# Layer B's attention: probabilities transposed one key block ahead of their products, work for later head pairs in smaller parts

## The chip, the cores and the metric

The kernel runs on one core of one Trainium2 chip. The metric is the time of one execution on the device in microseconds (us). The core's engines are TensorE (PE in the profile; PEld is its weight load), VectorE (DVE), ScalarE (ACT), GpSimd (POOL) and SyncE (SP); each runs its own instructions in their order and waits for the others at semaphores.

## What is computed

A trunk of two layers over 1024 tokens of width 1024: layer A (sparse attention and an MLP), then layer B (attention with shared keys and values, and an MLP). The change touches the attention of layer B alone:

```python
k_shared, v_shared = mla_shared_kv(rms_norm(h, kv_norm), w_dkv, ...)   # 16 heads, keys 96 wide, values 64 wide
...
q = (rms_norm(h @ w_dq, q_lora_gain) @ w_uq).reshape(b, s, B_HEADS, QK_DIM)
q = rope_tail(rms_norm(q, q_gain), cos, sin)
logits = jnp.einsum('bqhd,bshd->bhqs', qb, k).astype(jnp.float32) * (QK_DIM ** -0.5)
logits = jnp.where(mask, logits, NEG)          # key chunk of 64 not later than the query's
p = jax.nn.softmax(logits, axis=-1).astype(v.dtype)
out = jnp.einsum('bhqs,bshd->bqhd', p, v)
```

Products are float32 in effect: an operand is split into a high and a low part, and each product is made of two or three matmuls.

## The kernel before

The 16 heads of layer B go in eight pairs j = 0 to 7. A pair has four **quarters** (half, h): half 0 are queries 0 to 511, half 1 queries 512 to 1023, and h is the head of the pair. They go in the order (0,0), (1,0), (0,1), (1,1) (the last pair ends with (1,1), (0,1)).

For each quarter `logits` makes four rows of blocks, i = 0 to 3: scores of 128 queries against their admissible keys (tile `blps`, L938, two PSUM banks in turn), their negated copy with the least value on VectorE (`bpr`, L939), the exponential on ScalarE (L942), the reciprocal of the sum on VectorE (L943), and the scaling on GpSimd (L944). `values` then goes over the quarter's key blocks sb (4 for half 0, 8 for half 1): up to four transposes of probabilities into a PSUM bank `bpt` (L957), a copy of the high part on ScalarE (`bph`, L88), the low part on VectorE (`bpl`, L88), and two products with the values into `bpo` (L962), first that of the high part, then that of the low. `output` adds the quarter into `res` with a copy `btmp` on ScalarE (L971) and an add on VectorE (L972).

The loop runs `logits` of a quarter beside `values` of the quarter before it, step by step, and strews between them the quarter's list in `plan`: work for later pairs, which is one long step each. `kv_a` makes keys and values of 256 tokens (12 matmuls into `pukv`, L750; copies and four squares with their sums on ScalarE, `ksq`; a root on GpSimd, `y_bk`, L81; scaling into `ktok` on VectorE). `kv_b` transposes them (`pkt`, L775). `q_a` makes queries of 256 tokens (18 matmuls into `puq`, L794; a copy and four squares on ScalarE, `bqsq`), `q_b` norms and rotates 512 of them (`y_bq` and three products of `qtok` on GpSimd, L813 to L818), `queries_t` transposes them (`pqt`, L825). Transposes of probabilities and this work share four PSUM banks (tag `pt`).

The code is not the order on the chip: the program is built with a scheduler that places the written steps anew on every engine, by its own estimate of their durations (`schedule_with_timeline_sim`). What stands where is therefore shown below from the built program.

## Time and profile before

| what | value |
|---|---|
| median of 3 runs | 2685.81 us (2684.93 to 2688.60) |
| the profiled execution, its own time | 2684.85 us |
| its span from first to last instruction | 2683.0 us |
| mean granted clock of TensorE | 0.984 |
| TensorE busy | 2532.4 us (94%), 13354 matmuls |
| its weight loads busy | 2148.5 us (80%) |
| VectorE busy | 1521.1 us (57%) |
| ScalarE busy | 1232.2 us (46%) |
| GpSimd busy | 1024.1 us (38%) |

The profile is of one execution. An engine's busy time is the union of its instructions. A matmul's end is modelled, so that a busy TensorE is not one at its peak. Idle time is put down to what ended last. The attention of layer B stands at 1446 to 1888 us of the span.

### The profile page before, as it was taken

To read this page: it belongs to the slowest core of one execution; us is meant where nothing else is said; L and a number is where in the kernel's file an instruction comes from. 1 tells how busy PE (TensorE), PEld (TensorE's weight loads), DVE (VectorE), ACT (ScalarE), POOL (GpSimd) and SP (SyncE) were. 2 spreads that over 40 slices of the span, in tenths; PEclk is the share of its full clock that TensorE was granted. 3 is DMA by queue.
4 is the path that set the end of the run, shared out by engine and by line. 5 is a ranking of instruction groups with operands and counts; after the bars stand their busy time and mean duration, and the time that the engine had idled before them with its cause. 6 is when DMAs were issued, how large, how long until landed. Compare 5 with 4: busy or idle time off the path is not lost.

```text
span 2683.0 us, 36853 instructions
## 1 busy us (share of the span) xinstructions
PE 2532.4 (94%) x13354; PEld 2148.5 (80%) x13354; DVE 1521.1 (57%) x3655; ACT 1232.2 (46%) x2989; POOL 1024.1 (38%) x756
## 2 busy tenths in 40 slices
PE   6997799999989999999998999998999999999999
PEld 5897678888768888888888788887778888888887
DVE  5798754999869861222257878897422232222223
ACT  4575744333357764243345777787222222222221
POOL 2235635443556535343324555555121212222120
PEclk9998999999999999999999999999999999999999
DMA  7202323222232223233210000002210101111111
GB/s 157 54 24 60 99 92 97 94 99 90 79 110 68 60 82 127 84 120 106 77 33 11 10 14 10 14 5 80 102 32 32 63 32 63 47 48 48 48 47 63
DMA packets 122293, 173.03 MB, mean 64 GB/s; under 512 B 12752, under 2 KB 101104, under 8 KB 122112
## 3 DMA queue, kind: packets, MB, share of 16 engines
q1 hardware_dynamic: 122112, 170.69, 20.5%
q8 instruction: 105, 1.72, 0.3%
q14 instruction: 76, 0.62, 0.1%
HBM read 159.13 MB, written 11.53 MB: 64 GB/s over the span
## 4 chain that ended last, share of the span: by engine, by line
PE 71%; DVE 7%; DMA 3%; ACT 3%; POOL 2%; issue 2%; SPq 0%; POOLq 0%; DVEq 0%; ACTq 0%
PE pd L1190 25%; PE pu L1120 25%; PE pwo L1066 3%; PE pwoa L1066 2%; PE blps L938 2%; PE bpo L962 2%; PE puq L794 2%; PE po L572 1%; PE ppt L566 1%; PE lps L543 1%; PE pcq L853 1%; PE pukv L750 1%; DVE bpr L939 1%; PE bpt L957 1%; PE pck L853 1%
## 5 line engine op out<-in xcount | busy, mean ns | idle before, releaser
L88 POOL TENSOR_TENSOR dl<-rd,dh 128x1024 fp32r<-128x1024 f32 x96 | 232.4, 2429 | 728.2 <-PE pu L1120 369.3
L1191 DVE TENSOR_TENSOR res<-res,pd 128x1024 f32<-128x1024 f32 x192 | 234.2, 1220 | 419.1 <-PE pd L1190 419.1
L1120 PE MATMUL pu<-mxh,uh 128*128 128x512 f32 (+1 forms) x1056 | 405.4, 384 | 2.4 <-DVE mxl L88 2.4
L1120 PE MATMUL pu<-mxl,uh 128*128 128x512 f32 (+1 forms) x1056 | 404.9, 383 | 0.0
L1120 PE MATMUL pu<-mxh,ul 128*128 128x512 f32 (+1 forms) x1056 | 404.9, 383 | 0.0
L1190 PE MATMUL pd<-dh,hh 128*128 128x512 f32 x1024 | 398.6, 390 | 5.1 <-DVE res L1191 3.1
L1190 PE MATMUL pd<-dl,hh 128*128 128x512 f32 x1024 | 398.5, 389 | 0.0
L1190 PE MATMUL pd<-dh,hl 128*128 128x512 f32 x1024 | 392.9, 389 | 1.6 <-DVE hl L88 1.6
L88 DVE TENSOR_TENSOR hl<-pu,hh 128x512 fp32r<-128x512 f32 (+1 forms) x132 | 88.8, 674 | 407.6 <-ACT hh L88 407.6
L88 ACT CAST dh<-rd 128x1024 fp32r<-128x1024 f32 x96 | 99.1, 1051 | 476.1 <-PE pd L1190 422.5
L88 POOL TENSOR_TENSOR ul<-ru,uh 128x1024 fp32r<-128x1024 f32 x96 | 231.9, 2418 | 167.2 <-ACT uh L88 166.9
L1177 ACT ACTIVATE pu<-pu 128x512 f32<-128x512 f32 (+1 forms) x132 | 75.0, 569 | 433.2 <-PE pu L1120 427.7
L1120 PEld LDWEIGHTS pu<-mxh,uh 128*128 128x128 f32 x1056 | 199.1, 189 | 41.7 <-DVE mxl L88 2.9
L1120 PEld LDWEIGHTS pu<-mxl,uh 128*128 128x128 f32 x1056 | 198.9, 188 | 39.0
L1120 PEld LDWEIGHTS pu<-mxh,ul 128*128 128x128 f32 x1056 | 199.0, 188 | 38.7
L1190 PEld LDWEIGHTS pd<-dh,hh 128*128 128x128 f32 x1024 | 192.3, 188 | 46.5 <-DVE res L1191 4.0
L1190 PEld LDWEIGHTS pd<-dh,hl 128*128 128x128 f32 x1024 | 192.2, 188 | 42.1 <-DVE hl L88 2.2
L1190 PEld LDWEIGHTS pd<-dl,hh 128*128 128x128 f32 x1024 | 192.3, 188 | 39.7
L444 DVE TENSOR_SCALAR_CACHE_REDUCE both<-score,cand 128x1024 f32<-128x1024 f32 (+1 forms) x192 | 181.2, 944 | 5.0
L944 POOL TENSOR_SCALAR bpr<-bpr,bsm 128x640 f32<-128x640 f32 (+7 forms) x128 | 98.4, 772 | 96.4 <-DVE bsm L943 55.9
L554 POOL TENSOR_SCALAR lg<-lg,sm 128x256 f32<-128x256 f32 (+7 forms) x128 | 99.4, 783 | 76.7 <-DVE sm L553 54.0
L88 ACT CAST uh<-ru 128x1024 fp32r<-128x1024 f32 x96 | 99.9, 1044 | 30.4 <-DMA ru<-in_mlp_w_up_dram 28.4
(374 smaller groups left out, 5982.0 us busy)
## 6 DMA issues: line engine op xcount, KB each, us to landing
ru<-in_mlp_w_up_dram SPq DMA_DIRECT2D x48, 1024.0 KB, 5.4
rd<-in_mlp_w_down_dram SPq DMA_DIRECT2D x48, 1024.0 KB, 4.9
bm<-near_d SPq DMA_DIRECT2D x56, 256.0 KB, 2.7
res<-in_x_dram SPq DMA_DIRECT2D x16, 512.0 KB, 6.3
wor_a<-in_a_w_o_dram SPq DMA_DIRECT2D x16, 512.0 KB, 3.6
wr_q<-in_a_w_in_dram SPq DMA_DIRECT2D x8, 512.0 KB, 8.7
x<-res SPq DMA_DIRECT2D x8, 512.0 KB, 2.6
wor_b<-in_b_w_o_dram SPq DMA_DIRECT2D x8, 512.0 KB, 3.6
```

The costliest lines, as they stand in the source:

```text
L88: return self.nc.scalar.copy(h, src), (engine or self.nc.vector).tensor_sub(l, src, h)
L444: nc.vector.tensor_scalar(scratch[0][0][:, :s.shape[-1]], s, cand[:, j:j + 1], None, op0=ALU.is_ge, op1=ALU.add, accum_out=cnt[:, j:j + 1])
L554: nc.gpsimd.tensor_scalar(lg[:, :S], lg[:, :S], rs, 1.0, op0=ALU.mult, op1=ALU.mult)
L794: nc.tensor.matmul(ps[:, 192 * u:192 * u + 192], a[:, kb, tsl], b[:, kb], start=(kb == 0 and i == 0), stop=(kb == 2 and i == 2))
L853: nc.tensor.matmul(ps, a[:, kb], b[:, kb], start=(kb == 0 and i == 0), stop=(kb == KB - 1 and i == 2))
L938: nc.tensor.matmul(lps, q[0:rows, tsl], k[0:rows, h, c:c + a], start=(m == 0), stop=(m == 2))
L944: nc.gpsimd.tensor_scalar(pr, pr, sm[:, 3:4], 1.0, op0=ALU.mult, op1=ALU.mult)
L1066: nc.tensor.matmul(open_ps[n], x[:, kb], w[:, kb, ns], start=(kb == 0 and i == 0), stop=(kb == KB - 1 and i == 2))
L1120: nc.tensor.matmul(pu, a[:, kb], b[:, kb, c0:c1], start=(kb == 0 and i == 0), stop=(kb == KB - 1 and i == 2))
L1177: nc.scalar.activation(pu, pu, AF.Relu)
L1190: nc.tensor.matmul(pd[:, ns], a[:, tsl], b[:, ns], start=(f == 0 and k == 0), stop=(f == NS - 1 and k == 2))
L1191: nc.vector.tensor_add(res[:, tb], res[:, tb], pd)
```

## The change

`values` is cut in two: `turn_probs` makes the transposes of a key block and their high and low parts, and `values` only the two products. `attended` writes the steps of a quarter: the transposes of key block sb + 1 stand ahead of the products of block sb, and a share of the other work stands between the two. `bph` and `bpl` have three buffers in place of two. `kv_a` and `q_a` go in two parts (128 tokens each), so that other steps may stand between their halves; copies and squares come behind the second part. The lists of `plan` are spread anew over the four quarters, and the last quarter's products are written with the output projection between them in the same manner. The number of instructions on each engine stays.

```diff
@@ -739,17 +739,21 @@
                 keys[j] = stream(w_ukv[:, :, 256 * j:256 * j + 256], 2, 256, "uk", j, 1)
                 vals[j] = (a2 if j % 2 else j2).tile([P, NB, 2, P], F32R, name=f"bv{j}", tag="bv", bufs=1)
 
-            def kv_a(j, t2):
+            def kv_a(j, t2, parts=(0, 1)):
 
                 wh, wl = keys[j]
-                ps = filler((2, 2, P), f"pukv{j}_{t2}")
-                for u in range(2):
+                if 0 in parts:
+                    keys["ps", j, t2] = filler((2, 2, P), f"pukv{j}_{t2}")
+                ps = keys["ps", j, t2]
+                for u in parts:
                     tsl = slice((2 * t2 + u) * P, (2 * t2 + u + 1) * P)
                     for kb in range(2):
                         for i, (a, b) in enumerate(((ckh, wh), (ckh, wl), (ckl, wh))):
                             nc.tensor.matmul(ps[:, 256 * u:256 * u + 256], a[:, kb, tsl], b[:, kb],
                                              start=(kb == 0 and i == 0), stop=(kb == 1 and i == 2))
-                ps = ps.rearrange("p (a b c) -> p a b c", a=2, b=2)
+                if 1 not in parts:
+                    return
+                ps = keys.pop(("ps", j, t2)).rearrange("p (a b c) -> p a b c", a=2, b=2)
                 kt = j2.tile([P, 2, 2, 96], F32, name=f"ktok{j}_{t2}", tag="ktok", bufs=3)
                 ss = j2.tile([P, 2, 2], F32, name=f"bkss{j}_{t2}", tag="bkss")
                 nc.scalar.copy(kt[:, :, :, 0:64], ps[:, :, :, 0:64])
@@ -779,20 +783,25 @@
             def q_w(j):
                 keys["q", j] = stream(w_uq[:, :, 192 * j:192 * j + 192], 3, 192, "uq", j, 2)
 
-            def q_a(j, t2):
+            def q_a(j, t2, parts=(0, 1)):
 
                 half = t2 // 2
-                if t2 % 2 == 0:
+                if t2 % 2 == 0 and 0 in parts:
                     qtok[j, half] = j2.tile([P, 4, 2, 96], F32, name=f"qtok{j}_{half}", tag="qtok", bufs=4)
                     sums[j, half] = j2.tile([P, 4, 2], F32, name=f"bqss{j}_{half}", tag="bqss", bufs=4)
                 wh, wl = keys["q", j]
-                ps = filler((2, 192), f"puq{j}_{t2}")
-                for u in range(2):
...
+                if 1 not in parts:
+                    return
+                del keys["qs", j, t2]
                 b = 2 * (t2 % 2)
                 q = qtok[j, half][:, b:b + 2]
                 nc.scalar.copy(q, ps.rearrange("p (u h c) -> p u h c", u=2, h=2))
@@ -944,29 +953,48 @@
                 nc.gpsimd.tensor_scalar(pr, pr, sm[:, 3:4], 1.0, op0=ALU.mult, op1=ALU.mult)
                 probs[j, half, h, i] = pr
 
-            def values(j, half, h, sb):
+            parts = {}
+
+            def turn_probs(j, half, h, sb):
+
                 nm = f"{j}_{half}_{h}"
-                nb = 4 * half + 4
-                if sb == 0:
-                    outs[j, half, h] = pp.tile([P, 512], F32, name=f"bpo{nm}", tag="po", bufs=2)
-                po = outs[j, half, h]
                 i0 = max(0, sb - 4 * half)
                 c = slice(i0 * P, 512)
                 pt = pp.tile([P, 4, P], F32, name=f"bpt{nm}_{sb}", tag="pt", bufs=4)
                 for i in range(i0, 4):
                     nc.tensor.transpose(pt[:, i], probs[j, half, h, i][:, sb * P:(sb + 1) * P], self.ident)
-                ph = a2.tile([P, 512], F32R, name=f"bph{nm}_{sb}", tag="bph")
-                pl = a2.tile([P, 512], F32R, name=f"bpl{nm}_{sb}", tag="bpl")
+                ph = a2.tile([P, 512], F32R, name=f"bph{nm}_{sb}", tag="bph", bufs=3)
+                pl = a2.tile([P, 512], F32R, name=f"bpl{nm}_{sb}", tag="bpl", bufs=3)
                 self.split_evac(ph[:, c], pl[:, c], pt.rearrange("p a b -> p (a b)")[:, c])
-                for n, m in enumerate((ph, pl)):
+                parts[j, half, h, sb] = ph, pl
+
+            def values(j, half, h, sb):
+                nb = 4 * half + 4
+                if sb == 0:
+                    outs[j, half, h] = pp.tile([P, 512], F32, name=f"bpo{j}_{half}_{h}", tag="po", bufs=2)
+                po = outs[j, half, h]
+                c = slice(max(0, sb - 4 * half) * P, 512)
+                for n, m in enumerate(parts.pop((j, half, h, sb))):
                     nc.tensor.matmul(po[:, c], vals[j][:, sb, h], m[:, c], start=(sb == 0 and n == 0), stop=(sb == nb - 1 and n == 1))
+
+            def attended(last, other):
+
+
+                n = 4 * last[1] + 4
+                steps = [lambda: turn_probs(*last, 0)]
+                for sb in range(1, n + 1):
+                    if sb < n:
+                        steps += [lambda sb=sb: turn_probs(*last, sb)]
+                    steps += other[(sb - 1) * len(other) // n:sb * len(other) // n]
+                    steps += [lambda sb=sb: values(*last, sb - 1)]
+                return steps + [lambda: output(*last)]
 
             def output(j, half, h):
 
                 po = outs.pop((j, half, h))
                 mine, other = slice(64 * h, 64 * h + 64), slice(64 - 64 * h, 128 - 64 * h)
...
-                tmp = a2.tile([P, 4, P], F32, name=f"btmp{j}_{half}_{h}", tag="bph")
+                tmp = a2.tile([P, 4, P], F32, name=f"btmp{j}_{half}_{h}", tag="bph", bufs=3)
                 p4 = po.rearrange("p (a b) -> p a b", a=4)
                 nc.scalar.copy(tmp[mine], p4[other])
                 nc.vector.tensor_add(dst, p4[mine], tmp[mine])
@@ -976,16 +1004,17 @@
 
             NJ = H // 2
             plan = [
-                [(q_b, 1, 1), (kv_w, 1), (kv_b, 0, 2), (queries_t, 0, 1, 1), (kv_b, 0, 3), (q_a, 2, 0)],
-                [(kv_a, 1, 0), (queries_t, 1, 0, 0), (q_a, 2, 1)],
-                [(q_w, 3), (kv_a, 1, 1), (kv_b, 1, 0), (q_b, 2, 0), (queries_t, 1, 1, 0), (q_a, 2, 2)],
-                [(kv_a, 1, 2), (kv_b, 1, 1), (queries_t, 1, 0, 1), (kv_a, 1, 3), (q_a, 2, 3)],
+                [(kv_b, 0, 2), (q_a, 2, 0), (q_b, 1, 1), (kv_w, 1), (kv_b, 0, 3), (queries_t, 0, 1, 1), (q_a, 2, 1)],
+                [(kv_a, 1, 0), (queries_t, 1, 0, 0)],
+                [(q_w, 3), (q_a, 2, 2), (kv_b, 1, 0), (q_b, 2, 0), (kv_a, 1, 1), (queries_t, 1, 1, 0), (kv_a, 1, 2)],
+                [(kv_b, 1, 1), (queries_t, 1, 0, 1), (kv_a, 1, 3), (q_a, 2, 3)],
             ]
 
             def fill(j, u):
 
                 steps = first_plan[u] if j == 0 and u in first_plan else plan[u]
-                return [lambda s=s: s[0](j + s[1], *s[2:]) for s in steps if j + s[1] < NJ]
+                steps = [s + p for s in steps if j + s[1] < NJ for p in ([((0,),), ((1,),)] if s[0] in (kv_a, q_a) else [()])]
+                return [lambda s=s: s[0](j + s[1], *s[2:]) for s in steps]
 
             first_plan = {
                 0: [(q_b, 0, 1), (kv_a, 0, 3), (kv_b, 0, 2), (q_b, 1, 0), (queries_t, 0, 1, 0), (kv_w, 1), (kv_b, 0, 3), (q_w, 2),
@@ -1002,13 +1031,11 @@
                 for u, (half, h) in enumerate(((0, 0), (1, 0), (0, 1), (1, 1)) if j < NJ - 1 else ((0, 0), (1, 0), (1, 1), (0, 1))):
                     extra = fill(j, u)
                     first = [lambda i=i: logits(j, half, h, i) for i in range(4)]
-                    second = []
-                    if last is not None:
-                        second = [lambda sb=sb: values(*last, sb) for sb in range(4 * last[1] + 4)] + [lambda: output(*last)]
-                    steps = []
-                    for i in range(max(len(first), len(second))):
-                        steps += first[i:i + 1] + second[i:i + 1]
-                    weave(steps, extra)
+
+                    n = 4 * last[1] + 4 if last else 4
+                    other = woven(first, extra[:len(extra) * 4 // n]) + extra[len(extra) * 4 // n:]
+                    for step in attended(last, other) if last else other:
+                        step()
                     last = (j, half, h)
                     if j == NJ - 1 and u == 0:
                         st_j.close()
@@ -1025,7 +1052,8 @@
                 split = [op.tile([P, KB, P], F32R, name=f"bo{k}{tb}", tag=f"bo{k}") for k in "hl"]
                 tail += self.out_proj(tb, split, wo, res, x1[tb],
                                       lambda n, tb=tb: pp.tile([P, 512], F32, name=f"pwob{tb}_{n}", tag="lps", bufs=2))
-            weave([lambda sb=sb: values(*last, sb) for sb in range(4 * last[1] + 4)] + [lambda: output(*last)], tail)
+            for step in attended(last, tail):
+                step()
             st_b.close()
             st_w.close()
 
```

Everything ahead of layer B's attention, and what follows it behind the first rows of the output projection, has the same order on every engine as before.

In the built program TensorE stands so around the end of quarter (1,0) of pair 3, where its last probabilities (`bpr3_1_0_2`, `bpr3_1_0_3`) are turned. First before: the end of the twelve matmuls of a part of the next keys, then transposes.

```order
L750 MATMUL pukv4_1_16706<-ukh4_16332,ckh_12282 128x256
L750 MATMUL pukv4_1_16706<-ukl4_16331,ckh_12282 128x256
L750 MATMUL pukv4_1_16706<-ukh4_16332,ckl_12283 128x256
L957 MATMUL bpt3_1_0_2_16742<-ident_58,bpr3_1_0_0_16466 128x128
L957 MATMUL bpt3_1_0_0_16650<-ident_58,bpr3_1_0_2_16554 128x128
L957 MATMUL bpt3_1_0_1_16685<-ident_58,bpr3_1_0_2_16554 128x128
L957 MATMUL bpt3_1_0_2_16742<-ident_58,bpr3_1_0_1_16493 128x128
```

Then the same transposes of `bpr3_1_0_2` in the changed program: scores of the next quarter stand ahead of them, and no `pukv4_1`, which has moved to between the products of quarter (1,0); so have the four transposes of `pkt4_0`, which before stood ahead of its first product.

```order
L947 MATMUL blps3_0_1_3_0_16767<-kth1_13728,qth01_13732 128x512
L947 MATMUL blps3_0_1_3_0_16767<-ktl1_13730,qth01_13732 128x512
L947 MATMUL blps3_0_1_3_0_16767<-kth1_13728,qtl01_13736 128x512
L965 MATMUL bpt3_1_0_0_16639<-ident_58,bpr3_1_0_2_16566 128x128
L965 MATMUL bpt3_1_0_1_16648<-ident_58,bpr3_1_0_2_16566 128x128
L965 MATMUL bpt3_1_0_2_16670<-ident_58,bpr3_1_0_2_16566 128x128
L965 MATMUL bpt3_1_0_3_16705<-ident_58,bpr3_1_0_2_16566 128x128
```

GpSimd at the same place, before: the four scalings of quarter (1,0) (`bpr3_1_0_0` to `_3`) with two roots between them, and the norming of the next queries (`qtok5_0`) behind them.

```order
L944 TENSOR_SCALAR bpr3_1_0_0_16466<-bpr3_1_0_0_16466,bsm3_1_0_0_16467 128x640
L81 TENSOR_TENSOR y_bk4_0_16535<-ms_bk4_0_16534,mhalf_65 128x4
L944 TENSOR_SCALAR bpr3_1_0_1_16493<-bpr3_1_0_1_16493,bsm3_1_0_1_16494 128x768
L944 TENSOR_SCALAR bpr3_1_0_2_16554<-bpr3_1_0_2_16554,bsm3_1_0_2_16555 128x896
L81 TENSOR_TENSOR y_bq5_0_16793<-ms_bq5_0_16792,mhalf_65 128x8
L944 TENSOR_SCALAR bpr3_1_0_3_16585<-bpr3_1_0_3_16585,bsm3_1_0_3_16586 128x1024
L944 TENSOR_SCALAR bpr3_0_1_0_16639<-bpr3_0_1_0_16639,bsm3_0_1_0_16640 128x128
L813 TENSOR_TENSOR qtok5_0_16436<-qtok5_0_16436,y_bq5_0_16793 128x768
```

And after: both roots and `qtok5_0` stand ahead of the scalings of `bpr3_1_0_2` and `bpr3_1_0_3`. It is so in pairs 1 to 5.

```order
L953 TENSOR_SCALAR bpr3_1_0_0_16511<-bpr3_1_0_0_16511,bsm3_1_0_0_16512 128x640
L81 TENSOR_TENSOR y_bq5_0_16802<-ms_bq5_0_16801,mhalf_65 128x8
L953 TENSOR_SCALAR bpr3_1_0_1_16536<-bpr3_1_0_1_16536,bsm3_1_0_1_16537 128x768
L81 TENSOR_TENSOR y_bk4_0_16601<-ms_bk4_0_16600,mhalf_65 128x4
L822 TENSOR_TENSOR qtok5_0_16331<-qtok5_0_16331,y_bq5_0_16802 128x768
L953 TENSOR_SCALAR bpr3_1_0_2_16566<-bpr3_1_0_2_16566,bsm3_1_0_2_16567 128x896
L953 TENSOR_SCALAR bpr3_1_0_3_16612<-bpr3_1_0_3_16612,bsm3_1_0_3_16613 128x1024
L826 TENSOR_TENSOR qtok5_0_16331<-qtok5_0_16331,tn_12289 128x8x64
```

ScalarE in the middle of quarter (1,0)'s products, before: the casts of key blocks 3 to 7 (`bph3_1_0_3` to `_7`) stand close together; the copy and the squares of the next queries come behind them.

```order
L88 CAST bph3_1_0_3_16775<-bpt3_1_0_3_16770 128x512
L88 CAST bph3_1_0_4_16786<-bpt3_1_0_4_16781 128x512
L88 CAST uqh6_16672<-uqr6_0_16673 128x192
L88 CAST bph3_1_0_5_16811<-bpt3_1_0_5_16807 128x384
L88 CAST qth10_13733<-pqt4_1_0_16826 96x512
L88 CAST bph3_1_0_6_16820<-bpt3_1_0_6_16817 128x256
L88 CAST bph3_1_0_7_16835<-bpt3_1_0_7_16833 128x128
L88 CAST uqh6_16672<-uqr6_1_16677 128x192
```

And after: the copy of `puq5_2` and its squares stand between the casts of blocks 3, 4 and 5.

```order
L88 CAST bph3_1_0_3_16710<-bpt3_1_0_3_16705 128x512
L807 COPY qtok5_1_16714<-puq5_2_16716 128x384
L811 ACTIVATE bqsq5_2_0_0_16757,bqss5_1_16715<-qtok5_1_16714 128x96
L811 ACTIVATE bqsq5_2_0_1_16759,bqss5_1_16715<-qtok5_1_16714 128x96
L811 ACTIVATE bqsq5_2_1_0_16761,bqss5_1_16715<-qtok5_1_16714 128x96
L88 CAST bph3_1_0_4_16743<-bpt3_1_0_4_16738 128x512
L811 ACTIVATE bqsq5_2_1_1_16763,bqss5_1_16715<-qtok5_1_16714 128x96
L88 CAST bph3_1_0_5_16781<-bpt3_1_0_5_16777 128x384
```

## Rows read from the trace of the kernel before

**Rows 1.** Attention stretch: length, busy PE, PEld, DVE, ACT, POOL; granted clock, DMA.
```profile
1446.00:1888.00 442.00, 403.14 (x2604) 346.53 (x2604) 362.28 (x1112) 334.04 (x1091) 242.38 (x254) 0.97 0.07 21
```

**Rows 2.** TensorE's groups in 1446:1888, by line: busy, mean ns | idle before, releasers.
```profile
L962 PE MATMUL bpo<-bpl,bv 128*128 128x512 f32 x192 | 77.2, 403 | 11.6 <-DVE bpl L88 10.9
L962 PE MATMUL bpo<-bph,bv 128*128 128x512 f32 x192 | 72.1, 376 | 8.3 <-ACT bph L88 8.3
```

**Rows 3.** Waits in 1446:1888: us in total, times, longest.
```profile
ACT bph L88 <- DVE bpl L88: 14.0, 14, 2.5
DVE bpl L88 <- PE bpo L962: 9.1, 7, 5.5
```

**Rows 4.** Pair 3 in six stretches A to F, columns as in rows 1.
```profile
1644.68:1652.65 7.97, 7.18 (x50) 6.11 (x48) 7.05 (x26) 7.89 (x33) 5.67 (x7) 1.00 0.00 0
1652.65:1661.67 9.02, 8.30 (x56) 6.93 (x57) 7.38 (x20) 4.67 (x13) 5.05 (x7) 1.00 0.11 30
1661.67:1673.17 11.50, 10.60 (x72) 9.14 (x70) 8.51 (x26) 9.85 (x41) 3.90 (x5) 1.00 0.02 5
1673.17:1681.45 8.28, 7.58 (x52) 6.25 (x50) 7.44 (x30) 6.77 (x24) 4.85 (x6) 1.00 0.00 0
1681.45:1690.76 9.31, 8.34 (x57) 6.91 (x57) 6.60 (x16) 5.24 (x14) 6.49 (x8) 1.00 0.11 31
1690.76:1701.04 10.28, 9.65 (x67) 8.48 (x65) 8.60 (x29) 9.19 (x38) 3.60 (x5) 1.00 0.00 1
```

**Rows 5.** Pair 2 in the same six stretches, A to F.
```profile
1589.61:1597.54 7.93, 7.73 (x54) 6.50 (x52) 7.09 (x28) 7.38 (x27) 7.19 (x8) 1.00 0.00 0
1597.54:1606.01 8.47, 8.23 (x57) 6.89 (x56) 6.82 (x19) 4.37 (x11) 4.24 (x6) 1.00 0.10 25
1606.01:1618.37 12.36, 10.12 (x58) 8.95 (x57) 7.56 (x26) 9.04 (x33) 3.72 (x6) 0.86 0.03 9
1618.37:1627.03 8.66, 8.60 (x62) 7.41 (x60) 7.50 (x28) 8.15 (x32) 5.47 (x6) 1.00 0.01 3
1627.03:1635.04 8.01, 7.93 (x58) 7.01 (x58) 5.93 (x17) 5.01 (x13) 6.19 (x8) 1.00 0.12 33
1635.04:1644.68 9.64, 9.29 (x65) 8.42 (x64) 8.68 (x29) 8.30 (x31) 4.09 (x5) 1.00 0.01 2
```

**Rows 6.** TensorE in order of time, stretch A of pair 3.
```profile
1644.68 0.40 PE L938 MATMUL blps<-kth,qtl 96*128 96x512 f32 x1
...
1645.73 0.33 PE L750 MATMUL pukv<-ukh,ckh 128*128 128x256 f32 x1
...
1647.19 0.71 PE L957 MATMUL bpt<-ident,bpr 128*128 128x128 f32 x5
...
1652.65 0.50 PE L962 MATMUL bpo<-bpl,bv 128*128 128x512 f32 x1 [0.80 <-DVE bpl L88]
```

**Rows 7.** GpSimd in order of time, same stretch.
```profile
1648.10 1.46 POOL L944 TENSOR_SCALAR bpr<-bpr,bsm 128x1024 f32<-128x1024 f32 x2
```

**Rows 8.** GpSimd's groups in 1500:1858, shapes apart: busy, mean ns | idle before.
```profile
L81 POOL TENSOR_TENSOR y_bk<-ms_bk,mhalf 128x4 f32<-128x4 f32 x26 | 26.8, 1031 | 26.0 <-DVE ms_bk L80 21.9 <-DVE bsm L943 3.7
L944 POOL TENSOR_SCALAR bpr<-bpr,bsm 128x1024 f32<-128x1024 f32 x15 | 17.0, 1134 | 4.9 <-DVE bsm L943 3.5 <-DVE t_bq L83 1.2
L944 POOL TENSOR_SCALAR bpr<-bpr,bsm 128x896 f32<-128x896 f32 x15 | 16.2, 1077 | 10.4 <-PE bpo L962 4.8 <-DVE bsm L943 2.6 <-DVE t_bk L82 1.3
L813 POOL TENSOR_TENSOR qtok<-qtok,y_bq 128x768 f32<-128x768 f32 x11 | 16.2, 1469 | 4.4 <-DVE y_bq L84 2.8 <-DVE ms_bk L80 1.0 <-DVE bsm L943 0.6
```

**Rows 9.** ScalarE's groups in 1500:1858 that a part of the next keys brings.
```profile
L761 ACT ACTIVATE ksq<-ktok 128x64 f32<-128x64 f32 x104 | 26.2, 262 | 0.0
L761 ACT ACTIVATION_READ_ACCUMULATOR ksq<-ktok 128x1 f32 x104 | 21.2, 203 | 0.0
```

**Rows 10.** A small VectorE step of tile y_bk in 1500:1858: duration ns min/median/max.
```profile
L84 DVE SCALAR_TENSOR_TENSOR y_bk<-t_bk,y_bk x26: 144/161/1293, 1506.5 to 1833.3; 128x4 f32<-128x4 f32 x26
```

**Rows 11.** VectorE in order of time, stretch A of pair 3: a copy of 512 scores.
```profile
1650.12 0.67 DVE L939 CUSTOM_DVE_ANT_0 bpr<-blps,zero 128x512 f32<-128x512 f32 x1
```

More of the change, by code (lines that the diff above doesn't have):

```diff
@@ L788, in q_a @@
                 wh, wl = keys["q", j]
-                ps = filler((2, 192), f"puq{j}_{t2}")
-                for u in range(2):
+                if 0 in parts:
+                    keys["qs", j, t2] = filler((2, 192), f"puq{j}_{t2}")
+                ps = keys["qs", j, t2]
+                for u in parts:
                     tsl = slice((2 * t2 + u) * P, (2 * t2 + u + 1) * P)
```

## The prediction

> **What bounds the kernel now.** The change moves only layer B's attention, so I first asked the view of busy times by stretch for that part. In its 442.0 us TensorE is busy for 403.1, VectorE for 362.3, ScalarE for 334.0 [rows 1]. TensorE is the busiest, and it stands still for 442.0 - 403.1 = 38.9 us. Since every other stage keeps its order, these 38.9 us are all that the change can give by removing waits, 1.4% of the span; its matmuls stay the same in number and shape.
>
> Then the groups by line, for TensorE alone in that stretch: who ends its idle time. The products of probabilities and values hold half of it: 11.6 us ahead of the low parts, which VectorE makes, and 8.3 us ahead of the high parts, which ScalarE casts [rows 2]. These are the waits that transposing one key block ahead speaks to.
>
> Third, the list of waits for the engines that make these parts. ScalarE waited 14.0 us in 14 places to overwrite a high part that VectorE had not yet read, and VectorE 9.1 us for a low part's buffer [rows 3]. Both are waits for the second buffer; the change gives a third.
>
> Last, one pair of heads cut into six stretches, to see where the engines are unevenly loaded [rows 4, 5]. A goes from the last score matmul of quarter (1,0) to its first low product, B to its last product, C to the last score matmul of quarter (1,1), D to that quarter's first low product, E to its last product, F to the last score matmul of the next pair's (1,0). Pairs 2 and 3 are shown, the full period takes 55.07 and 56.36 us (sum of the six). TensorE's idle time, length less busy time, is in pair 2 0.20, 0.24, 2.24, 0.06, 0.08, 0.35 and in pair 3 0.79, 0.72, 0.90, 0.70, 0.97, 0.63. As means: A 0.50, B 0.48, C 1.57, D 0.38, E 0.52, F 0.49, together 3.9 us a pair. Now look at ScalarE: in A it is busy 7.38 of 7.93 and 7.89 of 7.97, in B only 4.37 of 8.47 and 4.67 of 9.02, in E 5.01 of 8.01 and 5.24 of 9.31. The quarter ends, where the softmax of the last row must come through, carry the fillers' ScalarE work too; the long runs of products have room for it.
>
> **The change, part by part.** The sum is made against the profiled execution, 2684.85 us; its span is 2683.0, and it lies 0.96 us below the median of 2685.81. The period repeats for pairs 1 to 6, six times.
>
> *Look-ahead and third buffer, in the product runs B and E.* A product pair no longer waits with its own transposes just ahead, and a cast finds a free buffer. The gain is between nothing (if VectorE, busy 7.38 of 9.02 in B, is what paces the run) and all idle time of both, 0.48 + 0.52 = 1.0 us a pair. Against it stands that the copy and the squares of `q_a` now stand between the casts of these runs; four squares with their sums take 4 x (0.262 + 0.203) = 1.9 us [rows 9], and ScalarE has 9.02 - 4.67 = 4.3 us free in B. So I take the upper end, nearest to what ScalarE's room allows: -1.0 x 6 = -6.0 us. For the waits of rows 3 I add nothing of their own: they come before the idle time of the products and are in it.
>
> *Stretch C.* Here the four-block quarter (0,1) is turned while ScalarE does the squares of `kv_a`; it is busy 9.85 of 11.50 us. One part of `kv_a` now goes earlier, into B, and takes 1.9 us of squares away. TensorE's idle time is 1.57 on the mean, and in pair 2 a wait of that stretch comes with a granted clock of 0.86 in it, where the neighbours have 1.00 (part of the time at 1.2 GHz in place of 2.4). Bounds: 0 and all 1.57. The order in the built program does not lengthen the way from transposes to products here, so I take a half: -0.78 x 6 = -4.7 us.
>
> *Stretch D.* The 18 matmuls of a `q_a` part come into it, work for TensorE while the last softmax of (1,1) is made. Bounds 0 and 0.38; I take the upper: -0.4 x 6 = -2.3 us. F: only its idle 0.49 could go; with 9.19 of 10.28 us on ScalarE I take 0.
>
> *Stretch A, which pays.* The twelve matmuls of `pukv` that stood there are gone; they took from 1645.73 to 1647.19, 1.46 us [rows 6]. And GpSimd scales the last two rows later. Before, the scaling of row 3 began at 1648.10 [rows 7] and takes 1.13 [rows 8], so it was ready 1649.23 - 1644.68 = 4.55 us after the last score matmul. Afterwards the root `y_bk` waits for a VectorE step that stands behind the copy of the first half of the last scores. Such a copy takes 0.67 us [rows 11]; it can begin when the second half's three matmuls do, the last of which is the mark, so its end and the small step behind it lie at about 0.45 us after the mark (an estimate from these two rows). Behind it the root 1.03, the norming of `qtok` 1.47, and the scalings 1.08 and 1.13 follow on GpSimd: 0.45 + 4.71 = 5.2 us, 0.6 later than before. So A loses between 0 (ScalarE, freed of 1.9 us, lets the chain come through that much sooner) and 0.6 + 1.46 = 2.1 us. I take the middle, 1.0, in the five pairs 1 to 5 that have this order on GpSimd: +5.0 us.
>
> *Nothing at the ends.* The start of the attention has the same first rows; at the end the last products and the first rows of the output projection change places, the same matmuls in both orders, and TensorE has them all to do before the MLP.
>
> Sum: -6.0 - 4.7 - 2.3 + 5.0 = -8.0 us, 2676.9 for the profiled execution, and with its 0.96 us to the median **2677.8 us**, 0.3% faster. A difference under 0.2%, some 5.4 us, I count as none; it is about what a measurement of this kernel can tell.
>
> **The rivals.**
>
> *It is already done (no change).* The scheduler had hoisted transposes before: in stretch A three key blocks are turned ahead of the first product. Then the written look-ahead moves little, the product runs are paced by VectorE (7.38 of 9.02 in B, 6.60 of 9.31 in E; the second figure speaks against), and what is left is -4.7 in C and +5.0 in A: 2684.85 - 4.7 + 5.0 + 0.96 = 2686 us. Chance 0.24.
>
> *GpSimd becomes what TensorE waits for (slower).* In A all 2.1 us of the loss show in five pairs, +10.3 us, and the other stretches give nothing, since each pair's later quarters begin that much later: 2684.85 + 10.3 + 0.96 = 2696 us. For it speaks that in pair 3 TensorE came to its first low product with 0.80 us of waiting already [rows 6], and that GpSimd is a single queue with each root ahead of a scaling. Against it, that GpSimd is busy only 5.67 of 7.97 us there. It decides if the other five stretches together give less than 10.3 / 6 = 1.7 us a pair. Chance 0.25.
>
> *Small VectorE steps held by GpSimd.* A step on 128 x 4 values takes 0.161 us as a rule and up to 1.293 [rows 10]. The norming of `qtok` on GpSimd now lies beside these steps in A; if one in each of five pairs is held, 1.13 x 5 = 5.7 us, and with the rest as forecast the time is 2683.5 us, no change. The Trainium skill, SBUF — State Buffer, section Who interferes with whom, says that a VectorE instruction with two inputs in SBUF and a GpSimd instruction that reads SBUF exclude each other for the whole instruction. The long case of that row agrees with it; no row here shows the two side by side. Chance 0.08.
>
> **How the numbers follow.** The forecast has 0.43, the rivals 0.24, 0.25 and 0.08. So faster 0.43, the same 0.32, slower 0.25. The fast end takes all idle time of the six stretches, 3.9 x 6 = 23.6 us, less the 5.0 of A: 2667. The slow end reaches most of the way to 2696, to 2693; about two in ten lie outside. The forecast's own range, if it holds, is 2667 to 2680.
>
> **What would show it.** TensorE's idle time ahead of the low products should fall from 11.6 to 6 or less, and ahead of the high ones from 8.3 to about 5; ScalarE's 14.0 us of waiting for VectorE should go. By stretch, ScalarE in B should be busy for 6 us or more and B and E run without idle TensorE. A should show idle time ahead of the transposes of the last row with GpSimd's scaling as what ended it, about 1 us. Wrong it would be if transposes wait for GpSimd by more than 1.7 us a pair, if the idle time only moves from the low products to the transposes or scores, or if VectorE is as little idle in B and E as TensorE.

## The result, and the profile after

| what | before | after |
|---|---|---|
| median of 4 runs each | 2687.20 us | 2715.38 us (2709.33 to 2721.51) |
| ratio, 95% interval | | 1.0107 [1.0093, 1.0121] |
| the profiled execution, its own time | 2684.85 us | 2712.77 us |
| its span | 2683.0 us | 2711.0 us |
| mean granted clock of TensorE | 0.984 | 0.978 |

The change makes the kernel 1.1% slower; 0.3% faster was forecast, and the range ended at 2693 us.

The view of busy times for layer B's attention after (columns as in [rows 1]):

```profile
1449.50:1915.50 466.00, 410.62 (x2605) 353.12 (x2605) 368.54 (x1114) 336.34 (x1094) 242.02 (x255) 0.95 0.07 20
```

Against [rows 1] the stretch is 466.0 - 442.0 = 24.0 us longer, of the 27.9 us between the two profiled executions. (Of the rest, some stands at the attention's end, told below, and some ahead of it, where the order is the same: the first score matmul starts at 1447.9 us before and 1451.5 after, and between 1447.9 and 1458.2 in all the profiled executions here.) TensorE's idle time is 466.0 - 410.6 = 55.4 us where it was 38.9, so 16.5 us more. The other 7.5 us are TensorE's busy time for the same matmuls, at a mean clock of 0.95 where it was 0.97.

TensorE's groups in that part, after (busy, mean ns | idle time ahead, what ended it):

```profile
L947 PE MATMUL blps<-kth,qth 104*128 104x128 f32 (+2 forms) x192 | 79.2, 414 | 29.8 <-DVE bsm L948 26.1 <-ACT kth L88 1.0 <-DVE res L1000 0.8
L978 PE MATMUL bpo<-bpl,bv 128*128 128x512 f32 x192 | 76.3, 398 | 3.5 <-DVE bpl L88 3.5
L978 PE MATMUL bpo<-bph,bv 128*128 128x512 f32 x192 | 73.8, 385 | 8.1 <-ACT bph L88 7.6
```

The low parts' products wait 3.5 us where they waited 11.6 [rows 2]. What came in its place is the first line: score matmuls wait 29.8 us, 26.1 of them for a PSUM bank whose scores VectorE has not yet copied (its step reading out the least value, `bsm`, comes with the copy). The same line of the kernel before is this one:

```profile
L938 PE MATMUL blps<-kth,qth 104*128 104x128 f32 (+2 forms) x192 | 76.8, 401 | 6.0 <-DVE bsm L939 5.6
```

Pair 3 in the six stretches A to F, after (columns as in [rows 1], against [rows 4]), and A and B of pair 2 below it (against [rows 5]):

```profile
1654.61:1665.47 10.86, 6.91 (x36) 5.63 (x35) 9.91 (x30) 5.69 (x15) 8.35 (x9) 0.90 0.00 0
1665.47:1676.13 10.66, 10.66 (x79) 9.87 (x79) 5.17 (x12) 7.24 (x31) 1.90 (x3) 0.94 0.06 18
1676.13:1685.86 9.73, 8.53 (x50) 6.54 (x49) 8.95 (x36) 7.76 (x25) 4.87 (x6) 1.00 0.05 13
1685.86:1695.53 9.67, 8.71 (x65) 7.69 (x63) 8.24 (x31) 9.23 (x36) 5.73 (x7) 1.00 0.00 0
1695.53:1705.11 9.58, 9.26 (x70) 8.16 (x69) 7.18 (x15) 5.40 (x18) 5.01 (x5) 1.00 0.10 30
1705.11:1713.72 8.61, 8.42 (x56) 7.53 (x56) 7.17 (x24) 7.93 (x30) 4.08 (x4) 1.00 0.00 0
...
1593.98:1605.24 11.26, 7.91 (x36) 6.34 (x35) 9.91 (x30) 5.68 (x15) 8.34 (x9) 0.70 0.00 0
1605.24:1617.05 11.81, 11.81 (x80) 11.00 (x79) 4.80 (x11) 6.49 (x26) 1.89 (x3) 0.85 0.07 18
```

A is where it goes wrong: 10.86 us long with TensorE busy for 6.91, and only 36 matmuls in it where there were 50. VectorE is busy for 9.91 of it. B now has 79 and 80 matmuls where it had 56 and 57. In it TensorE never stands still, but the granted clock is 0.94 in pair 3 and 0.85 in pair 2, and 0.70 in pair 2's A; before, both had 1.00 in both pairs.

VectorE in order of time in pair 3's A, then GpSimd and TensorE in the same time:

```profile
1657.09 1.01 DVE L82 TENSOR_TENSOR t_bk<-ms_bk,y_bk 128x4 f32<-128x4 f32 x1
...
1658.36 0.71 DVE L83 SCALAR_TENSOR_TENSOR t_bk<-t_bk,y_bk 128x4 f32<-128x4 f32 x1
...
1659.92 1.05 DVE L824 TENSOR_TENSOR rot<-qtok,sgq 128x128 f32<-128x128 f32 x1
1660.90 1.34 DVE L825 TENSOR_TENSOR rot<-qtok,sgq 128x128 f32<-128x128 f32 x1
1662.16 0.15 DVE L952 RECIPROCAL bsm<-bsm 128x1 f32<-128x1 f32 x1
1662.23 0.53 DVE L948 CUSTOM_DVE_ANT_0 bpr<-blps,zero 128x384 f32<-128x384 f32 x1
```

```profile
1656.61 1.47 POOL L822 TENSOR_TENSOR qtok<-qtok,y_bq 128x768 f32<-128x768 f32 x1
1658.06 1.01 POOL L953 TENSOR_SCALAR bpr<-bpr,bsm 128x896 f32<-128x896 f32 x1
1659.32 1.52 POOL L953 TENSOR_SCALAR bpr<-bpr,bsm 128x1024 f32<-128x1024 f32 x1 [0.25 <-DVE y_bk L84]
1660.81 1.28 POOL L826 TENSOR_TENSOR qtok<-qtok,tn 128x512 f32<-128x512 f32 x1
```

```profile
1659.30 0.60 PE L965 MATMUL bpt<-ident,bpr 128*128 128x128 f32 x4
1662.83 0.42 PE L947 MATMUL blps<-kth,qth 104*128 104x320 f32 x1 [2.93 <-DVE bsm L948]
```

Read the ends. `t_bk`, four values in each of 128 partitions, ends at 1658.10; GpSimd's `qtok` step ends at 1658.08. The second `t_bk` and the scaling of 896 columns both end at 1659.07. The two rotation products end at 1660.97 and 1662.24, GpSimd's steps beside them at 1660.84 and 1662.09. Each of the four VectorE steps ends within 0.15 us of the GpSimd step beside it. The copy of scores in the last VectorE line stands behind them, and TensorE, out of other work, waits 2.93 us for it. Such a wait, 2.13 to 2.93 us, stands at the same matmul in each of pairs 1 to 4. In pair 5 a wait of 2.67 us stands two groups of scores earlier, behind the three small steps of the root (`t_bk` twice, then `y_bk`), which last 1.22, 0.95 and 1.20 us there.

### The profile page after: what moved, and what is told of

It is laid out like the page before. It is cut to its first block, busy times and chain, and to the rows that moved or that the text cites. A ratio compares the mean times of both kernels' runs of the same rounds, so it can differ in the third digit from the quotient of the medians.

```text
span 2711.0 us, 36755 instructions
## 1 busy us (share of the span) xinstructions
PE 2548.0 (94%) x13354; PEld 2159.6 (80%) x13354; DVE 1524.4 (56%) x3655; ACT 1232.9 (45%) x2989; POOL 1025.3 (38%) x756
## 4 chain that ended last, share of the span: by engine, by line
PE 70%; DVE 9%; DMA 4%; POOL 2%; ACT 2%; issue 2%; SPq 0%; DVEq 0%; POOLq 0%; ACTq 0%
PE pd L1218 25%; PE pu L1148 25%; PE pwo L1094 3%; PE pwoa L1094 2%; PE blps L947 2%; DVE bpr L948 2%; PE puq L800 2%; PE po L572 2%; DMA ukr<-in_w_ukv_dram 1%; PE ppt L566 1%; PE bpo L978 1%; PE lps L543 1%; PE pcq L862 1%; PE bpt L965 1%; PE pck L862 1%
## 5 line engine op out<-in xcount | busy, mean ns | idle before, releaser
L951 ACT ACTIVATE bpr<-bpr,bsm 128x640 f32<-128x640 f32 (+7 forms) x128 | 99.5, 778 | 41.2 <-DVE bsm L948 32.1
```

What stands on the lines that cost most here:

```text
L951: nc.scalar.activation(pr, pr, AF.Exp, bias=least, scale=-1.0, accum_out=sm[:, 1:2])
```

## The experiments

**Theory one**, formed from these rows: the new lists put the queries' norming (GpSimd's `qtok`, VectorE's rotation) at the end of quarter (1,0), and look-ahead and halves take the matmuls out of it that had covered such waits; VectorE steps that read two SBUF tiles are held by GpSimd's steps, the copies of scores behind them come late, and TensorE starves. **Rivals**: GpSimd's later scaling is what counts; or the new lists or the halves by themselves, whatever VectorE does.

### Moving the steps

`dve_order` issues VectorE's rotation behind the copies of (0,1)'s scores (first two lines, around both products); `gp_order` issues GpSimd's first `qtok` product (L822) behind the scaling of (1,0)'s last row (last two).

```diff
+                    if half == 0 and (j - 2, 0, 1, 3) in copied:
+                        late.enter_context(tc.issue_after(copied[j - 2, 0, 1, 3].ins))
...
+                    if half == 0 and (j - 2, 1, 0, 3) in scaled:
+                        late.enter_context(tc.issue_after(scaled[j - 2, 1, 0, 3].ins))
```

> The changed kernel, with one order on VectorE pinned: the two steps rot of the next queries go behind the copies of the scores of quarter (0,1), in the pairs that have them. Theory one (VectorE's steps rot, held up by GpSimd to 1.05 and 1.34 us in pair 3, stand ahead of the copies that free the score banks, and TensorE waits for a bank): the 2.9 us wait of the score matmul falls by about 2.4 us in five pairs, -12 us, and with the clock that no longer falls some -14: near 2701 us. Theory two (the wait comes from the look-ahead as such, that is from transposes standing ahead of scores on TensorE): no change, 2715. Theory three (the new lists put too much work for VectorE into this place, whatever its order): VectorE is as busy, the wait moves to the first low products, 2710 to 2715.

> The changed kernel, with one order on GpSimd pinned: the three products of the next queries (qtok) go behind the scaling of the last probabilities of quarter (1,0). The scheduler then also places rot later on VectorE. Theory one: the held steps t_bk (1.01 and 0.71 us in pair 3) and rot become short, the copies of the scores come 3 to 4 us sooner, five pairs, -17 us: near 2698 us, lower than the run that moves rot alone. Theory two (look-ahead): 2715. Theory three (too much work here): 2710 to 2715.

`dve_order`: 2701.82 us, 1.0061 [1.0045, 1.0077]. `gp_order`: 2689.22 us, 1.0009 [1.0000, 1.0019]. Pair 3's A in `gp_order`, and then B:

```profile
1640.70:1647.70 7.00, 6.00 (x36) 4.53 (x34) 6.41 (x28) 5.42 (x14) 5.33 (x6) 1.00 0.00 0
1647.70:1657.84 10.14, 10.14 (x80) 9.44 (x79) 6.36 (x14) 7.45 (x31) 5.00 (x8) 1.00 0.07 19
```

With the same 36 matmuls A now takes 7.00 us in place of 10.86, at full clock. `dve_order` came out at theory one's figure, `gp_order` 9 us below it. The order on GpSimd makes nearly all of the loss, more than theory one priced. The edit both shortens VectorE's steps and brings the scaling forward, and this run does not part the two.

### The lists, the look-ahead and the halves apart

`old_plan` is after with the old lists; `plan_alone` is before with the new ones; `no_parts` is after with whole steps of `kv_a` and `q_a`; `ahead_alone` has look-ahead and third buffers with old lists and whole steps; `third_buffer` and `parts_alone` are before with that one part; `qa_back` is after with one entry of the lists moved back.

```diff
-                [(kv_b, 0, 2), (q_a, 2, 0), (q_b, 1, 1), (kv_w, 1), (kv_b, 0, 3), (queries_t, 0, 1, 1), (q_a, 2, 1)],
-                [(kv_a, 1, 0), (queries_t, 1, 0, 0)],
+                [(kv_b, 0, 2), (q_a, 2, 0), (q_b, 1, 1), (kv_w, 1), (kv_b, 0, 3), (queries_t, 0, 1, 1)],
+                [(kv_a, 1, 0), (queries_t, 1, 0, 0), (q_a, 2, 1)],
```

> The changed kernel with the lists of the kernel before: look-ahead, third buffer and smaller parts stay, the work is not spread anew. Theory one (the new lists bring the next queries' norming to the end of quarter (1,0)): the wait for score banks is gone and the shorter waits for low parts stay, 2675 to 2688 us. Theory two (look-ahead or parts are the cause): 2705 or more.

> The kernel before with the new lists alone: no look-ahead, two buffers, whole parts. Theory one: the norming of the next queries comes to the end of quarter (1,0) here too, TensorE waits there for score banks, 2700 us or more. Theory two (look-ahead or parts are the cause): 2683 to 2692 us.

> After with keys' and queries' steps whole again; look-ahead, third buffers and the new lists stay. GpSimd still has the products of the queries ahead of the scaling of the last row of (1,0), and TensorE 37 matmuls in stretch A (35 in after, 49 in before). Theory one: nothing that it names has changed, so the copies of scores are held as in after, 2708 to 2718 us. Rival (the halves delay ScalarE's squares and with them the norming, so that it falls into stretch A): the loss goes, 2680 to 2692 us.

> Look-ahead and third buffers alone: the old lists and whole steps. Theory one: the queries' norming lies outside stretch A, VectorE's held steps are not ahead of the scores there, so 2678 to 2684 us in spite of only 32 matmuls in stretch A; the wait for low parts falls from 11.6 to about 3 us. Rival (too few matmuls in stretch A are enough by themselves to lose): A is over 9 us long in pair 3 and the time above 2692 us.

> Before with three buffers for high and low parts and nothing else. If the missing third buffer was what the 14.0 us of ScalarE's waiting cost: TensorE's idle time ahead of low parts falls by half or more and the time is 2676 to 2681 us. Rival (the parts are paced by VectorE and the written order, the buffer only moves the place of waiting): ScalarE's waiting goes, the time stays at 2684 to 2688 us.

> Before with keys' and queries' steps in two halves and nothing else. The prediction gave the halves (with the look-ahead) B, C and D. Look-ahead and third buffers alone measured 0.9995, with the halves 0.9977. Theory: halves fill stretch D and shorten C by themselves, 2678 to 2683 us. Rival (they pay only where the look-ahead leaves places between transposes and products): 2685 to 2690 us.

> After with one entry of the new lists moved back: the queries' step (q_a, 2, 1) goes to the quarter (1,0) again. By the built order GpSimd then scales all rows of (1,0) before it norms the queries, and VectorE's rotation stands behind two copies of low parts. Theory one: this one entry carries the loss, so 2685 to 2692 us. Rival (the whole of the new lists does, by the matmuls that they take out of stretch A): over 2700 us.

| run | lists | look-ahead, third buffers | halves | us | ratio, 95% interval |
|---|---|---|---|---|---|
| plan_alone | new | no | no | 2683.25 | 0.9988 [0.9978, 0.9998] |
| no_parts | new | yes | no | 2722.87 | 1.0129 [1.0111, 1.0147] |
| after | new | yes | yes | 2715.38 | 1.0107 [1.0093, 1.0121] |
| qa_back | new but one | yes | yes | 2683.40 | 0.9989 [0.9979, 0.9998] |
| ahead_alone | old | yes | no | 2687.12 | 0.9995 [0.9986, 1.0005] |
| old_plan | old | yes | yes | 2680.18 | 0.9977 [0.9965, 0.9988] |
| parts_alone | old | no | yes | 2687.14 | 1.0006 [0.9994, 1.0019] |
| third_buffer | old | third buffers only | no | 2687.53 | 0.9997 [0.9985, 1.0008] |

The new lists alone do not lose: theory one's figure for `plan_alone` was a miss. Its pair 3 still has a long A, but with 60 matmuls in it, and B is short (7.60 us):

```profile
1638.54:1649.86 11.32, 9.56 (x60) 8.55 (x58) 10.12 (x31) 7.56 (x24) 8.12 (x10) 0.85 0.00 0
```

Nor does the look-ahead alone. It needs both, and one entry, `(q_a, 2, 1)`, turns the loss into no loss. The halves are not its cause: without them it is no smaller, though there the low parts' products wait 12.6 us again, so that not all of it need be the same loss. The third buffers alone gain nothing, nor do the halves alone: ScalarE's waiting for VectorE falls from 14.0 us [rows 3] to 7.2 with the third buffers, and the low parts' products wait as before, 12.2 us where it was 11.6 [rows 2].

```profile
ACT bph L88 <- DVE bpl L88: 7.2, 9, 1.2
```

```profile
L962 PE MATMUL bpo<-bpl,bv 128*128 128x512 f32 x192 | 75.7, 394 | 12.2 <-DVE bpl L88 11.9
```

Theory one's ranges for `ahead_alone` (2678 to 2684 us) and `no_parts` (2708 to 2718) were misses too, and so was the gain expected of `third_buffer` and of `parts_alone`; `qa_back` and `old_rot_gpsimd` (below) fell 1.6 and 0.6 us under their ranges.

### The hold itself

Three kernels keep the order of after (`one_input` and `reduce_all` with small moves) and change the form of the held steps; the sine factor, and in `reduce_all` the keys' root refinement, are left out.

```diff
-                nc.vector.tensor_tensor(rot[:, :, :, 0:16], q[:, :, :, 80:96], row(sgq[:, :, 0:16], 16), op=ALU.mult)
+                nc.vector.tensor_scalar(rot[:, :, :, 0:16], q[:, :, :, 80:96], 1.0, None, op0=ALU.mult)
...
+                nc.vector.tensor_reduce(rot.rearrange("p a b c -> p (a b) c")[:, :, 0:16], q.rearrange("p a b c -> p (a b) c")[:, :, 80:96].unsqueeze(3), axis=AX.X, op=ALU.add)
```

(the first + line in `one_input`, the second in `reduce_rot` and `reduce_all`, and the other half likewise)

> VectorE's two rotation steps (L824, L825) read one SBUF tile in place of two, by a scalar factor of 1.0; the sine factor is left out, so that the queries are not those of the reference. Theory one (VectorE steps with two SBUF inputs are held until the running GpSimd step ends, and the copies of scores behind them come late): the two steps take about 0.28 us each in place of 1.05 and 1.34, the copies in stretch A come some 1.8 us earlier, TensorE's idle time ahead of score matmuls falls from 29.8 to about 20 us (the roots' steps are still held), and the time is near 2703 us (2700 to 2707). Rival (the steps are late by their place in the order, not held): they stay above 0.9 us or the copies stay late, and the time is 2715 us as before the edit.

> VectorE's two rotation steps as sums over an axis of length one, which read one tile; the sine factor is left out, so that the queries are not those of the reference. The order of TensorE and GpSimd is that of after, row for row. The scalar form of the same steps was still 1.0 to 1.3 us long beside GpSimd's steps, so it did not take the hold away. The Trainium skill, SBUF — State Buffer, Who interferes with whom, says that a reduction never contends with GpSimd. If the hold is what costs (theory one): the two steps take some 0.25 us each, the copies of scores come about 1.9 us earlier in each of five pairs, TensorE's idle time ahead of score matmuls falls from 29.8 to about 20 us, and the time is 2702 to 2707 us. Rival (the copies are late for another reason, by their place): 2713 to 2720 us.

> As the run before, and the two steps behind each root of the keys (L82, L83) are such sums as well, so that the roots are not refined; the order on TensorE and GpSimd moves a little. They took 1.01 and 0.71 us in stretch A of after. Theory one: another 1.4 us in each of five pairs, 2695 to 2700 us. Rival (GpSimd's later steps are then what the scores' softmax waits for): no better than the run before, 2702 to 2707 us.

`one_input`: 2719.53 us, 1.0117 [1.0102, 1.0132], by its text the rival's time. The second rotation step in the attention, its duration as least, median and greatest ns, says why it decides nothing: in after, in `one_input`, and in `reduce_rot`:

```profile
L825 DVE TENSOR_TENSOR rot<-qtok,sgq x15: 279/1344/1381, 1456.0 to 1818.6; 128x128 f32<-128x128 f32 x15
```

```profile
L825 DVE TENSOR_SCALAR rot<-qtok x15: 213/1310/1318, 1462.6 to 1824.9; 128x128 f32<-128x128 f32 x15
```

```profile
L825 DVE TENSOR_REDUCE rot<-qtok x15: 269/276/279, 1456.3 to 1809.1; 128x128 f32<-128x128 f32 x15
```

The scalar form, with one tile to read, is held just as long; I had taken the number of inputs for the whole rule. The sum over an axis of one is not held in any of its 15 steps. The Trainium skill, SBUF — State Buffer, Who interferes with whom, says both: a `tensor_scalar` can take both of VectorE's ports, the second of which is shared with GpSimd, and a reduction on trn2 never contends. These three rows agree.

`reduce_rot`: 2703.04 us, 1.0061 [1.0046, 1.0076], 12.3 us less than after, with TensorE's, ScalarE's and GpSimd's order the same row for row. `reduce_all`: 2697.97 us, 1.0041 [1.0026, 1.0056], another 5.1 us. Both fell into theory one's ranges and outside the rivals'. In `reduce_rot` TensorE's idle time ahead of score matmuls is 23.3 us (29.8 in after, about 20 expected), and the score matmul of pair 3 waits 0.73 us where it waited 2.93; the copy that it waits for starts 1.86 us sooner in A, and the four transposes ahead of it take 0.93 us in place of 0.60, at a lower clock:

```profile
1655.28 0.63 PE L947 MATMUL blps<-kth,qth 104*128 104x320 f32 x1 [0.73 <-DVE bsm L948]
```

`reduce_all` did not get its 5.1 us in the way that was expected. Its two sums no longer read the root and take 0.15 us each, but the two steps behind them last longer instead, 0.54 and 1.21 us where they took 0.16 and 0.42 in `reduce_rot`, and the score matmul of pair 3 waits 0.80 us. What differs is the granted clock: in A of pair 3, `reduce_rot` and then `reduce_all` below the steps. So this run does not show what the two steps cost.

```profile
1649.13 0.54 DVE L84 SCALAR_TENSOR_TENSOR y_bk<-t_bk,y_bk 128x4 f32<-128x4 f32 x1
1649.70 1.21 DVE L769 TENSOR_TENSOR ktok<-ktok,y_bk 128x256 f32<-128x256 f32 x1
...
1648.92:1658.33 9.41, 7.66 (x37) 6.18 (x36) 8.11 (x30) 5.69 (x15) 8.15 (x9) 0.76 0.00 0
1646.17:1654.37 8.20, 6.24 (x36) 4.59 (x34) 7.49 (x30) 5.32 (x14) 7.18 (x8) 1.00 0.00 0
```

### A version that beats both

`old_rot_gpsimd` is `old_plan` with the rotation's two products on GpSimd (`eng` is GpSimd for every pair but the first), the same computation; `before_rot_gpsimd` is that edit in the kernel before.

```diff
-                nc.vector.tensor_tensor(rot[:, :, :, 0:16], q[:, :, :, 80:96], row(sgq[:, :, 0:16], 16), op=ALU.mult)
+                eng.tensor_tensor(rot[:, :, :, 0:16], q[:, :, :, 80:96], row(sgq[:, :, 0:16], 16), op=ALU.mult)
```

> The look-ahead, the third buffers and the parts with the old lists (2680.2 us), and the rotation's two products on GpSimd in place of VectorE, the same computation. There the second product still took 1.36 us beside GpSimd's and TensorE waited 1.0 us for the low part of the keys behind it, once in each of five pairs. Theory one: 2674 to 2678 us. Rival (GpSimd's two more steps a pair and half delay the scaling of probabilities by as much): 2680 to 2686 us.

> Before with the rotation's two products on GpSimd and nothing else. If the gain of that edit (6.8 us on the old lists with look-ahead) is the hold's and the hold stood in the kernel before as well: 2678 to 2682 us. Rival (before, TensorE had enough matmuls in the queue where the rotation is held, so nothing is won): 2684 to 2689 us.

`old_rot_gpsimd`: **2673.38 us, 0.9947 [0.9930, 0.9964]**, the fastest here. `before_rot_gpsimd`: 2679.59 us, 0.9975 [0.9964, 0.9986]. The two gains add: 0.9977 x 0.9975 = 0.9952. The kernel before had the hold too, and in one place a wait of TensorE behind it, since the low part comes next on VectorE:

```profile
1573.69 1.35 DVE L816 TENSOR_TENSOR rot<-qtok,sgq 128x128 f32<-128x128 f32 x1
1575.56 0.45 PE L962 MATMUL bpo<-bpl,bv 128*128 128x384 f32 x1 [1.52 <-DVE bpl L88]
```

But there only 4 of the 15 second products last over 1 us, and the built order moves a little with the edit. So how much of the two gains is the hold's is not shown.

## Why the prediction was wrong

**The waits that the look-ahead speaks to** were named rightly, and they went: low parts 11.6 to 3.5 us, as forecast (6 or less), and ScalarE's 14.0 us for VectorE are gone from the list of waits. The high parts stayed at 8.1, not about 5. But idle time moved to the score matmuls, 6.0 to 29.8 us, which is one of the prediction's own signs of being wrong. Part of it moves with the look-ahead and the third buffers alone: in `ahead_alone` the low parts' wait is 4.7 us and that of scores 15.0, and the time is that of the kernel before (0.9995).

```profile
L947 PE MATMUL blps<-kth,qth 104*128 104x128 f32 (+2 forms) x192 | 76.1, 398 | 15.0 <-DVE bsm L948 14.9
L978 PE MATMUL bpo<-bpl,bv 128*128 128x512 f32 x192 | 74.6, 389 | 4.7 <-DVE bpl L88 4.3
```

**B and E, -6.0.** TensorE's idle time fell from 0.48 and 0.52 to 0 and 0.26 on the mean of pairs 2 and 3, -4.4 us over six pairs. In B the clock took it back: at 0.94 and 0.85 it takes 10.66 and 11.81 us, where `gp_order` at 1.00 needs 10.14 and 10.15 for the same products and work. (The squares of the queries were priced by the keys' row, 1.9 us; their own, 0.273 and 0.188 us each, give 1.8, so that did not matter.)

**C, -4.7.** Idle 1.57 to 1.20, so -2.2. **D, -2.3** was of the wrong sign: idle 0.38 to 0.96, +3.5. One wait there is 0.63 us for the low part of the keys:

```profile
1694.77 0.63 PE L965 MATMUL bpt<-ident,bpr 128*128 128x128 f32 x4 [0.63 <-DVE ktl L88]
```

**F, 0**: 0.49 to 0.32, -1.0.

**A, +5.0 with a bound of 2.1 a pair, is the step that failed.** Its idle time went from 0.50 to 3.65, +3.15 a pair, 15.8 us over five. The lower clock comes on top: its 36 matmuls keep TensorE busy for 6.91 and 7.91 us in pairs 3 and 2, and for 6.00 and 6.02 in `gp_order` at full clock. The step followed one chain, from GpSimd's scaling to the transposes, and its bound was a bound of that chain. Transposes waited for GpSimd by 1.1 us in the whole attention. The next quarter's score matmuls, whose PSUM banks VectorE must empty, were not followed at all, nor how many other matmuls were left in A to cover a late copy.

**Nothing at the ends** was wrong as well, and had no row behind it. The first product of the next stage waits for ScalarE's cast of `mxh`, before and after:

```profile
1888.73 0.50 PE L1066 MATMUL pwo<-woh_b,mxh 128*128 128x512 f32 x1 [1.33 <-ACT mxh L88]
1915.44 0.50 PE L1094 MATMUL pwo<-woh_b,mxh 128*128 128x512 f32 x1 [2.77 <-ACT mxh L88]
```

Before, output-projection matmuls still stood behind the last product of values; after, that product comes last, and no matmul covers what must follow it up to that cast. The wait is 2.77 us in all eleven kernels here with the look-ahead and 0.83 to 2.00 in the five without it. From that matmul to the MLP's first it is 92.0 us after and 90.7 before. So the end costs some 2.7 us, in `old_plan` and `old_rot_gpsimd` too.

Read by pairs 2 and 3, the six stretches hold 11.7 of the 16.5 us of added idle time; the rest was not followed further than this end.

**The rivals.** "It is already done" put the time at 2686 us, which is what the look-ahead or the halves alone measure, and not the change. "GpSimd becomes what TensorE waits for" named the right stretch and sign, but the wait at the transposes did not come, and at 2696 us it was too small. "Small VectorE steps held" had the mechanism, and was priced at one step of 1.13 us a pair. Four are held in each of five pairs. In pairs 1 to 4 they take 1.01 + 0.71 + 1.05 + 1.34 = 4.11 us; unheld, as the two reduction runs show, 0.15 + 0.15 + 0.28 + 0.28 = 0.86. So the hold is 3.25 us a pair there, and in pair 5, where three of the four belong to the root, 3.6: some 16.6 us of VectorE's time. What it costs the kernel is shown for the rotation's products alone: `reduce_rot` gave back 12.3 us. The working took the row of a 4-value step for the price and did not ask which other steps of two SBUF tiles the new place brings beside GpSimd: the rotation's products.

**What stays open.** `reduce_all` is still 11 us above before, and `gp_order` gives back 26 of the 28 us. Between them lie 9 us. In `reduce_all` some of VectorE's steps are still long, and the scaling of probabilities still stands behind the norming; no run has that scaling alone moved, so its share is not shown. That the look-ahead needs the halves to gain (0.9995, 1.0006, and 0.9977 together) is measured and not explained.

## What to carry to other kernels

When a change moves GpSimd work, list the VectorE steps that land beside it, ask of each whether it reads two SBUF tiles or is a scalar step in SBUF, and price it at up to the length of the GpSimd step; then ask who stands behind it in VectorE's queue. A bound for a stretch is only as good as the chains that it follows: follow every engine's queue that feeds TensorE there, and count the matmuls that are left to cover a late one, at the ends of the changed part too. Parts of a change that cost nothing alone can cost 1% together, so run them apart and in pairs.

## What the runs showed of the hardware

A VectorE step on 128 x 4 values, 0.15 us elsewhere, lasted 1.01 us beside a GpSimd step and ended with it. A scalar step of one input was held as long as the product that it replaced (1310 and 1344 ns in the median), a reduction was not (276 ns).

A stretch with short waits can lose its clock, and the price is paid in the work behind it. TensorE's length, busy time and granted clock in pair 3 of after, the first stretch with the waits of A, and then in pair 2:

```profile
1655.50:1662.80 7.30, 3.38 (x19) 1.00 0.00 0
1662.80:1664.50 1.70, 1.67 (x8) 0.66 0.00 0
1664.50:1666.50 2.00, 2.00 (x8) 0.50 0.00 0
1666.50:1668.50 2.00, 2.00 (x19) 0.93 0.00 0
1668.50:1672.00 3.50, 3.50 (x25) 1.00 0.09 28
...
1593.98:1598.50 4.52, 3.50 (x21) 1.00 0.00 0
1598.50:1602.20 3.70, 1.36 (x6) 0.50 0.00 0
1602.20:1608.70 6.50, 6.50 (x26) 0.50 0.00 0
1608.70:1617.05 8.35, 8.35 (x66) 1.00 0.10 26
```

In pair 3 TensorE was busy for 3.38 of 7.30 us, all at the full clock of 2.4 GHz, and when its work came, the clock fell to 0.50, the lower level of 1.2 GHz. In pair 2 it fell ahead of the long wait, after 4.52 us with 3.50 of work and no wait over 0.48 us, and stayed there for 6.50 us of work without a gap. That is why B, without idle time, takes 0.5 and 1.7 us more than in `gp_order`; the rest by which it is longer than before is the work that the lists put there. The low clock is not tied to the long wait alone: with that wait at 0.73 us, `reduce_rot` still has 0.76 in A of pair 3.
